# A hybrid decoder layer on one core: projections shared out by the VectorE time of the attention units they stand beside, and three of them moved one phase later

## The chip, the cores and the metric

The kernel is one program on 1 core of one Trainium2 chip. The metric is device time in microseconds (us). The kernel before takes 1305.38 us (median of 3 runs, 1304.23 to 1305.52).

The engines are named as the profile names them: PE is TensorE (matmuls and transposes), PEld its weight load, DVE is VectorE, ACT is ScalarE, POOL is GpSimd, SP is SyncE, which issues the DMAs.

## The reference

One decoder layer, 1024 tokens by 1024 features in float32. One input projection feeds two groups of heads; their outputs go side by side through one output projection, then a layer norm and a gated feed-forward network with a second layer norm.

```python
h = x @ w_in                                    # q, k, v of both groups, and gates
o_diff = diff_attention(dq, dk, dv, ...)        # 4 heads: softmax(q1 k1) - lam * softmax(q2 k2), times v, rms_norm
o_nsa = nsa_attention(nq, ..., gates, ...)      # 8 heads in 2 key groups: compressed + selected + window of 512
mix = concatenate([o_diff, o_nsa]) @ w_out
x = layer_norm(alpha * x + mix)
x = layer_norm(alpha * x + (silu(x @ w_gate) * (x @ w_up)) @ w_down)
```

Every mixer is causal with ALiBi slopes. With 1024 tokens there are 16 selection blocks of 64 and 16 are selected, so the selected branch sees every past key.

## The kernel before, in words

**Arithmetic.** Each float32 operand is split into a high and a low part (a cast on ACT, line L81, and a subtraction on DVE or POOL, L83). A projection is three matmuls per tile, L116, L117 and L118 in `mm3`: high by high, low by high, high by low. They write the PSUM tiles `psM`; `big` and `slot` are buffers for weights and activations, `w` tiles stream through.

**Stages.** First x and the first weights are loaded and the first key group is made (to about 66 us). Then come ten *phases* of attention: four for the sparse heads, which go in pairs (`nsa`, pairs 0 to 3), and six for the differential heads 0 to 3 (`diff`), heads 2 and 3 in two parts each. From about 570 us the rest of the output rows and the feed-forward network run to the end.

**Units.** A sparse phase has 8 blocks of 128 queries with two units each: kind 0 is selected plus compressed, kind 1 is the window. A unit's *front* makes the scores on PE (L323, L326 into `psS`), adds the ALiBi distance and takes the row maximum on DVE (L329, L332, which fill `t` and `m`), exponentiates on ACT (L346) and scales by gate and denominator on POOL (L411). Its *back*, two units later (one later in two of the differential phases), transposes the probabilities on PE (L365 or L355 into `psT`), splits them into `pt` (ACT L81, DVE L83), and multiplies with the values on PE (L418, L426, L428, L481 into `psO`). The differential units combine their two softmaxes on DVE (L466) and POOL (L468), and every four of them are normalised (POOL L496, DVE L497), transposed (L500) and sent through memory (`mix_d`) to the output rows.

**Fillers.** The projections that later phases need are generators, one step per few matmuls: `vg_fill` (values of a sparse block), `qf` (queries of a pair), `kf` (keys of the second sparse group), `kdf`, `qdf`, `dvf` (keys, queries and values of the differential heads), `wo_copy` and `wo_fill` (the output weights, loaded and split), `out_fill` (output rows), `ln_fill`. `held_fill` emits the finish of four differential blocks if it is being held. A key filler ends in DVE work too (L171, two a half), a query filler in DMA moves through `q`.

**What sets the order.** A table `phases` gives for each phase its units, its fillers, how many units a back stands behind its front, a factor `ahead`, a priority and a number `passed`. While the program is written out, `pump` advances the fillers in the middle of each back: before the change in proportion to a unit's *size* (2 x blocks + 1 for sparse units, blocks + 1 in twos for differential ones), so that all the phase's projection matmuls are spread evenly over the sizes. The units still open at the end of a phase have size 0 in the next one, so no filler step stands beside them there. `passed` says past how many later score matmuls a projection may be moved up. A scheduler then puts the instructions of each engine in their final order, with the projections at lower priority (by 2000) than the attention units. Each engine runs its list in that order and waits where an input or a buffer isn't there.

Of the kernel before, what the change touches and what calls it, by code (L numbers as in the profile page):

```python
# [17 lines left out]
P = 128  # L18
# [7 lines left out]
NC = NCMP + 1  # L26
# [11 lines left out]
def layer_kernel(ctx: ExitStack, tc: tile.TileContext, xT, x, w_t, w_vg, w_dv, lam_in, subln,  # L38
# [105 lines left out]
    with ExitStack() as ctx_a:  # L144
# [155 lines left out]


        marks, passed = [], [None]

# [71 lines left out]
        def nsa_units(p, qt, K, V):  # L375
# [7 lines left out]
            def make(i, kind):  # L383
                nb = i + 1 if kind == 0 else min(i + 1, WIN_BLOCKS)
                j0 = i + 1 - nb
                width = nb * P
# [50 lines left out]

                return front, back, 2.0 * nb + 1

# [4 lines left out]
        def diff_units(h, qt, kd, V):  # L444
# [3 lines left out]
            def make(i):  # L448
# [22 lines left out]
                def back(fill):  # L471
# [15 lines left out]
                    done.append(i)  # L487
                    if len(done) == 4:
                        late.append(lambda: finish(orow, ss, state["r0", hf]))

# [16 lines left out]

                return front, back, 2.0 * (i + 1) + 1

# [284 lines left out]
        def held_fill():  # L794

            def steps():
                tc.cur_priority -= FILL_LATER
                finish_held()
                tc.cur_priority += FILL_LATER
                yield 0.0  # L800
            return steps, 0.0

# [4 lines left out]
            ([(nsa, 0, (2, 1, 0, 3, 4, 5, 6, 7))],  # L807
             [vg_fill(3), vg_fill(4), qf(0, 1), vg_fill(5), vg_fill(6), vg_fill(7), qf(1, 0), kf(0), kf(1)],
             2, 1.25, 80, 16),
            ([(nsa, 1, range(8))],  # L810
             [qf(1, 1), wo_copy(0), dvf(0, range(8)), qf(2, 0)], 2, 1, 80, 8),
            ([(nsa, 2, range(7))],
             [qf(2, 1), kdf(0, 0), wo_copy(1), qf(3, 0), kdf(0, 1)], 2, 1, 60, 8),
            ([(nsa, 2, (7,)), (nsa, 3, (1, 0, 2, 3, 5, 4, 6, 7))],
             [qf(3, 1), qdf(0, 0), kdf(1, 0), kdf(1, 1)], 2, 1, 60, 8),
            ([(diff, 0, (2, 1, 0, 3, 5, 4, 6, 7))],
             [qdf(0, 1), qdf(1, 0), dvf(1, range(4))], 1, 1.25, 200, None),
            ([(diff, 1, range(8))],
# [12 lines left out]
        def finish_unit(pump, later):  # L831
            held.extend(late)
            late.clear()
            if pending:
                back, base, size = pending.pop(0)
                tc.cur_priority += later
                back(lambda part: pump and pump(base + part * size))
                tc.cur_priority -= later
            finish_held()

        for parts, fillers, look, ahead, later, passed[0] in phases:
            units = [u for make, head, blocks in parts for u in make(head, blocks)]
            total = sum(u[2] for u in units[:-1])
            rate = sum(f[1] for f in fillers) / total * ahead
            queue = [f[0] for f in fillers]
            run = {"gen": None, "spent": 0.0}

            def step():

                if run["gen"] is None:  # L850
                    if not queue:
                        return False
                    run["gen"] = queue.pop(0)()
                tc.cur_priority += FILL_LATER
# [7 lines left out]

            def pump(at):
                while run["spent"] < at * rate and step():
                    pass

            at = 0.0
            for front, back, cost, needs in units:
                while not needs <= there:
                    assert step()  # L870
                    while run["gen"]:
                        step()
                front()
                pending.append((back, at, cost))
                while len(pending) > look:
                    finish_unit(pump, later)
                at += cost
            while step():
                pass

            pending = [(p[0], 0.0, 0.0) for p in pending]
        while pending or late:
# [388 lines left out]
```

## Time and profile before

| | |
|---|---|
| median of 3 runs | 1305.38 us |
| the profiled execution | 1305.84 us, span 1304.1 us, mean granted TensorE clock 0.999 |
| busy | PE 1286.2 us (99%), PEld 1107.8, DVE 917.8, ACT 652.1, POOL 464.1 |
| pair 0 | 66.4 to 149.3 us |
| pair 1 | 149.3 to 232.8 us |
| pair 2 | 232.8 to 312.0 us |
| pair 3 | 312.0 to 391.2 us |
| differential heads 0, 1 | 391.2 to 482 us |
| differential heads 2, 3 | 482 to 570 us |
| output rows, feed-forward | 570 to 1304 us |

A row of instructions in the trace has start, length, engine, line, operation, output and input names, shapes and count; where the engine was idle ahead of it, the idle time and what ended it stand in brackets. Matmuls overlap in the pipeline, and their shown ends are modelled, so that PE reads as busy almost throughout. A group row ends in busy time, mean ns of one, and the idle time just before its instructions. A row by stretches has the stretch, its length, and for PE, PEld, DVE, ACT and POOL the busy time with the number of instructions, then the granted clock, the DMA share and GB/s.

### The profile page before, as it was taken

How to read it: one execution, taken by the hardware profiler on the slowest of the kernel's cores; microseconds unless marked ns; L12 is line 12 of the kernel's file. 1: busy time of each engine (PE TensorE's matmuls, PEld its weight loads, DVE VectorE, ACT ScalarE, POOL GpSimd, SP SyncE). 2: the span in 40 equal slices, each digit the busy share in tenths (PEclk: the TensorE clock that was granted, in tenths of full speed). 3: DMA queues.
4: the chain of work that ended last, by engine and by line, in shares of the span. 5: the costliest groups of instructions: out<-in, count | busy, mean ns of one | idle time of the engine just before them, and what ended most of it. 6: DMA issues, size and time to landing. Idle time of an engine off the chain costs nothing.

```text
span 1304.1 us, 20490 instructions
## 1 busy us (share of the span) xinstructions
PE 1286.2 (99%) x6955; PEld 1107.8 (85%) x6955; DVE 917.8 (70%) x1963; ACT 652.1 (50%) x1398; POOL 464.1 (36%) x499
## 2 busy tenths in 40 slices
PE   9999999999999999999999999999999999999997
PEld 7998999988988889788887888888888888888886
DVE  5567867778778667774797677776766768555588
ACT  5366866868776566653353333333333335533330
POOL 4434534545435446643613313232231222000071
PEclk9999999999999999999999999999999999999999
DMA  9412012121112135623224566555555559768641
GB/s 354 132 31 62 22 35 62 49 48 48 35 55 70 50 94 149 218 82 113 81 76 149 180 232 228 194 178 173 174 170 185 187 179 346 259 200 291 195 168 65
DMA packets 86841, 183.13 MB, mean 140 GB/s; under 512 B 10576, under 2 KB 19152, under 8 KB 86608
## 3 DMA queue, kind: packets, MB, share of 16 engines
q1 hardware_dynamic: 86736, 181.82, 42.7%
q8 instruction: 55, 0.90, 0.3%
q14 instruction: 50, 0.41, 0.1%
HBM read 116.18 MB, written 57.15 MB: 133 GB/s over the span
## 4 chain that ended last, share of the span: by engine, by line
PE 91%; DVE 4%; DMA 2%; ACT 2%; issue 1%; POOL 0%; SPq 0%; DVEq 0%; ACTq 0%
PE psM L116 11%; PE psM L118 11%; PE psM L117 11%; PE psS L118 6%; PE psS L117 6%; PE psS L116 6%; PE psT L118 5%; PE psT L117 5%; PE psT L116 5%; PE psT L365 4%; PE psS L323 3%; PE psS L326 3%; PE psO L428 2%; PE psO L426 2%; PE psO L481 2%; PE psO L116 2%
## 5 line engine op out<-in xcount | busy, mean ns | idle before, releaser
L346 ACT ACTIVATE t<-t,m 128x384 f32<-128x384 f32 (+7 forms) x192 | 144.2, 752 | 65.4 <-DVE m L332 59.8
L411 POOL TENSOR_SCALAR t<-t,r,gates 128x640 f32<-128x640 f32 (+7 forms) x128 | 99.6, 783 | 180.5 <-DVE r L405 82.4
L116 PE MATMUL psM<-big,w 128*128 128x512 f32 x304 | 120.6, 397 | 0.6 <-DVE slot L171 0.3
L118 PE MATMUL psM<-big,w 128*128 128x512 f32 x304 | 120.1, 396 | 0.0
L117 PE MATMUL psM<-big,w 128*128 128x512 f32 x304 | 119.9, 394 | 0.0
L323 PE MATMUL psS<-slot,q 128*128 128x320 f32 (+10 forms) x304 | 111.8, 369 | 2.2 <-DVE m L332 2.0
L1019 POOL TENSOR_TENSOR half<-half,half 128x512 f32<-128x512 f32 x22 | 33.5, 1524 | 205.0 <-ACT half L1018 205.0
L83 DVE TENSOR_TENSOR pt<-psT,pt 128x512 fp32r<-128x512 f32 (+1 forms) x152 | 91.3, 615 | 13.1 <-ACT pt L81 11.7
L326 PE MATMUL psS<-slot,q 128*128 128x320 f32 (+10 forms) x304 | 99.5, 329 | 0.0
L81 ACT CAST pt<-psT 128x512 fp32r<-128x512 f32 (+1 forms) x152 | 77.3, 525 | 20.6 <-PE psT L365 10.0
L81 ACT CAST big<-slot 128x1024 fp32r<-128x1024 f32 (+1 forms) x54 | 54.4, 1018 | 66.2 <-DVE slot L1011 50.5
L83 DVE TENSOR_TENSOR op<-op 128x1024 fp32r<-128x1024 f32 x44 | 60.9, 1388 | 36.3 <-ACT op L81 35.8
L83 DVE TENSOR_TENSOR big<-slot,big 128x1024 fp32r<-128x1024 f32 (+1 forms) x54 | 63.5, 1182 | 30.5 <-ACT big L81 30.3
L365 PE MATMUL psT<-ident,t 128*128 128x128 f32 x528 | 83.8, 273 | 0.8 <-DVE pt L83 0.7
L81 ACT CAST op<-op 128x1024 fp32r<-128x1024 f32 x44 | 45.9, 1052 | 61.8 <-DMA op<-t_d 55.6
L428 PE MATMUL psO<-pt,slot 128*128 128x256 f32 x264 | 72.1, 294 | 0.1
L426 PE MATMUL psO<-pt,slot 128*128 128x256 f32 x264 | 71.8, 289 | 0.0
L332 DVE CUSTOM_DVE_ANT_0 t<-psS,dsel 128x384 f32<-128x384 f32 (+9 forms) x128 | 62.3, 493 | 13.4 <-PE psS L326 9.6
L1023 POOL TENSOR_TENSOR half<-half,half 128x512 f32<-128x512 f32 x22 | 36.5, 1659 | 99.0 <-DVE half L1022 98.8
L81 ACT CAST big<-big 128x1024 fp32r<-128x1024 f32 (+1 forms) x49 | 44.2, 912 | 45.6 <-DMA big<-t_d 34.0
L118 PEld LDWEIGHTS psM<-big,w 128*128 128x128 f32 x304 | 57.1, 188 | 11.4
L116 PEld LDWEIGHTS psM<-big,w 128*128 128x128 f32 x304 | 57.2, 188 | 11.1 <-ACT w L81 0.8
(371 smaller groups left out, 3971.3 us busy)
## 6 DMA issues: line engine op xcount, KB each, us to landing
a_d<-slot SPq DMA_DIRECT2D x77, 256.0 KB, 3.0
t_d<-slot SPq DMA_DIRECT2D x77, 256.0 KB, 2.2
q<-q SPq DMA_DIRECT2D x48, 256.0 KB, 2.9
slot<-in_w_up_dram SPq DMA_DIRECT2D x22, 512.0 KB, 3.8
slot<-in_w_down_dram SPq DMA_DIRECT2D x22, 512.0 KB, 3.9
op<-a_d SPq DMA_DIRECT2D x44, 256.0 KB, 3.5
op<-t_d SPq DMA_DIRECT2D x44, 256.0 KB, 4.0
big<-a_d SPq DMA_DIRECT2D x33, 256.0 KB, 2.9
```

Source lines behind the costliest of these rows:

```text
L81: nc.scalar.copy(hi, src)
L83: eng.tensor_sub(lo, src, hi.bitcast(F32))
L116: nc.tensor.matmul(acc, lhsT=ah, rhs=bh, start=first, stop=False, skip_group_check=more)
L117: nc.tensor.matmul(acc, lhsT=ah, rhs=bl, start=False, stop=False, skip_group_check=more)
L118: nc.tensor.matmul(acc, lhsT=al, rhs=bh, start=False, stop=last, skip_group_check=more)
L323: mm = nc.tensor.matmul(ps[:, :c + part], lhsT=q[0], rhs=k[:, ks], start=True, stop=False)
L326: nc.tensor.matmul(ps[:, :c + part], lhsT=q[1], rhs=k[:, ks], start=False, stop=True)
L346: nc.scalar.activation(t[:, :width], t[:, :width], AF.Exp, bias=m, scale=-1.0, accum_out=r)
L365: nc.tensor.transpose(tp[:rows, n * P:(n + 1) * P], s, ident)
L411: nc.gpsimd.tensor_scalar(t, t, r[:, c:c + 1], gates[:, i, gc:gc + 1], op0=ALU.mult, op1=ALU.mult)
L426: nc.tensor.matmul(po[:, :256], lhsT=v, rhs=pt[:, 0, n * 256:(n + 1) * 256], start=False, stop=False)
L428: nc.tensor.matmul(po[:, :256], lhsT=v, rhs=pt[:, 1, n * 256:(n + 1) * 256], start=False, stop=last)
```

## The change

Four edits, none of which adds or drops an instruction: each engine has the same work in total.

First, each unit carries an estimate of its own PE and DVE time, from the new helpers `streamed` and `row_ops`, instead of a size. A phase's filler steps are given to a unit by `share`: what PE work would even out the ratio of PE to DVE work over the phase, less the unit's own PE work, and never under 0.2.

Second, units left open at a phase's end keep their estimate, and get filler steps in the next phase; the last units of a phase, whose backs come in the next, don't count in it.

Third, the table. The second group's keys `kf(0)` and `kf(1)` go from pair 0 to pair 1; the first differential values `dvf(0)` with `wo_copy(0)` go from pair 1 to pair 2; the first differential keys `kdf(0, 0)`, `kdf(0, 1)` and `wo_copy(1)` go from pair 2 to pair 3; `kdf(1, 1)` goes from pair 3 to differential head 0. In pair 0 `ahead` goes from 1.25 to 1 and `passed` from 16 to 8.

Fourth, `held_fill` now waits in the queue of fillers until the first halves of all four differential heads are there, and takes the finishes itself.

```diff
+        def streamed(cols, n=1):
+            return n * max(0.105, cols / 2400 + 0.0125)
+        def row_ops(cols, n):
+            return n * 0.24 + 0.00104 * cols
...
-                return front, back, 2.0 * nb + 1
+                cols = width + (0 if kind else NC)
+                n = -(-cols // 512)
+                pe = n * streamed(cols / n, 4) + streamed(P, 2 * nb + 2 * (1 - kind)) + streamed(256, 2 * nb + 1 - kind)
+                dve = 2 * row_ops(width, n) + nb // 2 * 0.69 + nb % 2 * 0.42 + (0.58 if kind else 1.19)
+                return front, back, (pe, dve)
...
                     if len(done) == 4:
+                        there.add(("row", h, hf))
                         late.append(lambda: finish(orow, ss, state["r0", hf]))
...
-                return front, back, 2.0 * (i + 1) + 1
+                n = -(-width // 512)
+                pe = n * streamed(width / n, 4) + streamed(P, i + 1) + streamed(4 * P, i + 1)
+                dve = 2 * row_ops(width, n) + 0.00075 * width + 1.4
+                return front, back, (pe, dve)
...
                 tc.cur_priority -= FILL_LATER
+                held.extend(late)
+                late.clear()
                 finish_held()
                 tc.cur_priority += FILL_LATER
                 yield 0.0
-            return steps, 0.0
+            return steps, 0.0, {("row", h, 0) for h in range(4)}
...
             ([(nsa, 0, (2, 1, 0, 3, 4, 5, 6, 7))],
-             [vg_fill(3), vg_fill(4), qf(0, 1), vg_fill(5), vg_fill(6), vg_fill(7), qf(1, 0), kf(0), kf(1)],
-             2, 1.25, 80, 16),
+             [vg_fill(3), vg_fill(4), qf(0, 1), vg_fill(5), vg_fill(6), vg_fill(7), qf(1, 0)], 2, 1, 80, 8),
             ([(nsa, 1, range(8))],
-             [qf(1, 1), wo_copy(0), dvf(0, range(8)), qf(2, 0)], 2, 1, 80, 8),
+             [qf(1, 1), kf(0), kf(1), qf(2, 0)], 2, 1, 80, 8),
             ([(nsa, 2, range(7))],
-             [qf(2, 1), kdf(0, 0), wo_copy(1), qf(3, 0), kdf(0, 1)], 2, 1, 60, 8),
+             [qf(2, 1), wo_copy(0), dvf(0, range(8)), qf(3, 0)], 2, 1, 60, 8),
             ([(nsa, 2, (7,)), (nsa, 3, (1, 0, 2, 3, 5, 4, 6, 7))],
-             [qf(3, 1), qdf(0, 0), kdf(1, 0), kdf(1, 1)], 2, 1, 60, 8),
+             [qf(3, 1), wo_copy(1), kdf(0, 0), kdf(0, 1), qdf(0, 0), kdf(1, 0)], 2, 1, 60, 8),
             ([(diff, 0, (2, 1, 0, 3, 5, 4, 6, 7))],
-             [qdf(0, 1), qdf(1, 0), dvf(1, range(4))], 1, 1.25, 200, None),
+             [kdf(1, 1), qdf(0, 1), qdf(1, 0), dvf(1, range(4))], 1, 1.25, 200, None),
...
-                back, base, size = pending.pop(0)
+                back, work = pending.pop(0)
                 tc.cur_priority += later
-                back(lambda part: pump and pump(base + part * size))
+                back(lambda part: pump and pump(part, work))
...
-            total = sum(u[2] for u in units[:-1])
-            rate = sum(f[1] for f in fillers) / total * ahead
-            queue = [f[0] for f in fillers]
-            run = {"gen": None, "spent": 0.0}
+            beside = [p[1] for p in pending] + [u[2] for u in units][:-look]
+            given = sum(f[1] for f in fillers)
+            even = (given + sum(pe for pe, _ in beside)) / sum(dve for _, dve in beside)
+            share = lambda w: max(0.2, even * w[1] - w[0])
+            rate = given / sum(map(share, beside)) * ahead
+            queue = [(f[0], f[2] if len(f) > 2 else set()) for f in fillers]
+            run = {"gen": None, "spent": 0.0, "due": 0.0}
...
-                    if not queue:
+                    if not queue or not queue[0][1] <= there:
                         return False
...
-            def pump(at):
-                while run["spent"] < at * rate and step():
+            def pump(part, work):
+                while run["spent"] < run["due"] + part * share(work) * rate and step():
                     pass
+                if part > 0.999:
+                    run["due"] += share(work) * rate
```

The two places below show PE's order; a row has the line, the operation, output and input, the matmul's size and, behind an x, how many stand in a row. Lines from L307 on stand 8 or more lower in the changed kernel: L323 becomes L331, L326 L334, L365 L373, L426 L434, L428 L436, L355 L363, L481 L493 and L500 L513.

The first place is pair 0, block 6, where the selected unit's four score pieces of 480 columns (keys in slot_236) stand among the backs of the units before. Before:

```order
L428 MATMUL psO<-pt,slot_551 128x256
L323 MATMUL psS<-slot_236,q 128x480
L326 MATMUL psS<-slot_236,q 128x480
L365 MATMUL psT<-ident,pc 64x128
L365 MATMUL psT<-ident,t 128x128 x2
L323 MATMUL psS<-slot_236,q 128x480
L326 MATMUL psS<-slot_236,q 128x480
L365 MATMUL psT<-ident,t 128x128 x6
L365 MATMUL psT<-ident,pc 64x128
L323 MATMUL psS<-slot_236,q 128x480
L326 MATMUL psS<-slot_236,q 128x480
```

The same place now:

```order
L436 MATMUL psO<-pt,slot_551 128x256
L373 MATMUL psT<-ident,pc 64x128
L373 MATMUL psT<-ident,t 128x128 x2
L331 MATMUL psS<-slot_236,q 128x480
L334 MATMUL psS<-slot_236,q 128x480
L373 MATMUL psT<-ident,t 128x128 x6
L331 MATMUL psS<-slot_236,q 128x480
L334 MATMUL psS<-slot_236,q 128x480
L116 MATMUL psM<-big,w 128x512
L117 MATMUL psM<-big,w 128x512
L118 MATMUL psM<-big,w 128x512
L116 MATMUL psM<-big,w 128x512
```

Between the third and the fourth score piece there was no projection matmul (psM), and now nine stand there, of which the rows show the first four.

The second place is the end of the differential heads, between the transposes of two finished groups of four blocks (od), those of head 2's and of head 3's first half. Before:

```order
L116 MATMUL psM<-big,w 128x512
L355 MATMUL psT<-ident,t 128x128 x4
L481 MATMUL psO<-slot_5637,pt 128x128 x2
L355 MATMUL psT<-ident,t 128x128 x4
L323 MATMUL psS<-slot_6049,q 128x448
L326 MATMUL psS<-slot_6049,q 128x448
L323 MATMUL psS<-slot_6049,q 128x448
L326 MATMUL psS<-slot_6049,q 128x448
L117 MATMUL psM<-big,w 128x512
L118 MATMUL psM<-big,w 128x512
L116 MATMUL psM<-big,w 128x512
```

The same scores now, from head 2's transposes on:

```order
L513 MATMUL psT<-ident,od 128x128 x4
L363 MATMUL psT<-ident,t 128x128 x9
L331 MATMUL psS<-slot_5973,q 128x448
L334 MATMUL psS<-slot_5973,q 128x448
L493 MATMUL psO<-slot_5519,pt 128x128 x2
L363 MATMUL psT<-ident,t 128x128 x4
L331 MATMUL psS<-slot_5973,q 128x448
L334 MATMUL psS<-slot_5973,q 128x448
L331 MATMUL psS<-slot_5974,q 128x448
L334 MATMUL psS<-slot_5974,q 128x448
```

Before, 18 projection matmuls stand between the two transposes of od, four of them among these rows; now none does, and the next is that of the first output rows, behind head 3's transposes as before.

More of the change, by code (lines that the diff above doesn't have):

```diff
@@ L842, in layer_kernel @@
             units = [u for make, head, blocks in parts for u in make(head, blocks)]
-            total = sum(u[2] for u in units[:-1])
-            rate = sum(f[1] for f in fillers) / total * ahead
-            queue = [f[0] for f in fillers]
-            run = {"gen": None, "spent": 0.0}
+            beside = [p[1] for p in pending] + [u[2] for u in units][:-look]
[5 more added lines that the diff above has]
+            run = {"gen": None, "spent": 0.0, "due": 0.0}
             def step():
                 if run["gen"] is None:
-                    if not queue:
+                    if not queue or not queue[0][1] <= there:
                         return False
-                    run["gen"] = queue.pop(0)()
+                    run["gen"] = queue.pop(0)[0]()
                 tc.cur_priority += FILL_LATER
@@ L861, in step @@
                 return True
-            def pump(at):
-                while run["spent"] < at * rate and step():
-                    pass
-            at = 0.0
-            for front, back, cost, needs in units:
+            def pump(part, work):
+                while run["spent"] < run["due"] + part * share(work) * rate and step():
+                    pass
+                if part > 0.999:
+                    run["due"] += share(work) * rate
+            for front, back, work, needs in units:
                 while not needs <= there:
@@ L873, in layer_kernel @@
                 front()
-                pending.append((back, at, cost))
+                pending.append((back, work))
                 while len(pending) > look:
                     finish_unit(pump, later)
-                at += cost
             while step():
                 pass
-            pending = [(p[0], 0.0, 0.0) for p in pending]
         while pending or late:
```

## The prediction

> **What bounds the kernel now.** The page's first and fourth parts come first.
>
> ```profile
> PE 1286.2 (99%) x6955; PEld 1107.8 (85%) x6955; DVE 917.8 (70%) x1963; ACT 652.1 (50%) x1398; POOL 464.1 (36%) x499
> PE 91%; DVE 4%; DMA 2%; ACT 2%; issue 1%; POOL 0%; SPq 0%; DVEq 0%; ACTq 0%
> ```
>
> PE is on 91% of the chain that ended last, and every engine keeps its work. So the change can only win time in which PE waits inside the attention stage, and the next question is how much of that there is. The busy share hides it: a matmul is shown longer than it keeps PE. The timeline of PE, where no wait is shown, gives the true step from one start to the next.
>
> ```profile
> 301.38 0.60 PE L365 MATMUL psT<-ident,t 128*128 128x128 f32 x4
> 301.81 0.27 PE L365 MATMUL psT<-ident,pc 128*64 128x128 f32 x1
> ...
> 303.46 0.31 PE L326 MATMUL psS<-slot,q 128*128 128x320 f32 x1
> 303.61 0.39 PE L116 MATMUL psM<-big,w 128*128 128x512 f32 x1
> 303.84 0.40 PE L117 MATMUL psM<-big,w 128*128 128x512 f32 x1
> ...
> 305.56 0.28 PE L428 MATMUL psO<-pt,slot 128*128 128x256 f32 x1
> 305.68 0.28 PE L426 MATMUL psO<-pt,slot 128*128 128x256 f32 x1
> ```
>
> 512 columns cost 303.84 - 303.61 = 0.23 us though shown as 0.39; 320 cost 0.15; 256 cost 0.12; 128 cost (301.81 - 301.38) / 4 = 0.108. Sizes between go by columns (480: 0.21, 416: 0.19). Count times step is PE's *work* in a stretch; its length less that is time *lost*. Next the view by stretches, one for each sparse pair (stretch, length, then PE, PEld, DVE, ACT, POOL busy).
>
> ```profile
> 66.20:149.20 83.00, 82.14 (x539) 73.98 (x538) 60.48 (x231) 58.03 (x175) 32.08 (x48) 1.00 0.15 38
> 149.20:232.70 83.50, 83.35 (x631) 79.74 (x630) 58.67 (x209) 60.74 (x166) 38.08 (x55) 1.00 0.17 45
> 232.70:311.90 79.20, 78.33 (x512) 70.55 (x511) 60.92 (x214) 60.09 (x162) 36.45 (x55) 1.00 0.17 41
> 311.90:390.90 79.00, 78.80 (x510) 70.74 (x509) 59.25 (x211) 59.89 (x162) 36.67 (x53) 1.00 0.21 55
> ```
>
> Counting the matmuls of each stretch at their steps (ends taken where the pair's first scores start) gives work of 78.3, 81.7, 74.9 and 75.3 us, so 4.6, 1.8, 4.3 and 3.8 us are lost: 14.5 us. The same count gives 4.1 us for differential head 0, 1.6 for head 1 and some 7.5 for heads 2 and 3; from 570 us on the order hardly changes. All that can be had is thus under 28 us, 2%, and it is spread thin. VectorE is nowhere full over a pair (60.5 of 83.0), so the loss must be local. The worst spot is 119.8 to 138.2 us, blocks 5 and 6 of pair 0; the groups of PE there:
>
> ```profile
> L426 PE MATMUL psO<-pt,slot 128*128 128x256 f32 x19 | 5.3, 294 | 0.0
> L365 PE MATMUL psT<-ident,t 128*128 128x128 f32 x34 | 5.3, 272 | 0.0
> L428 PE MATMUL psO<-pt,slot 128*128 128x256 f32 x18 | 5.2, 312 | 0.0
> L323 PE MATMUL psS<-slot,q 128*128 128x320 f32 x9 | 3.3, 368 | 0.8 <-DVE m L332 0.8
> L326 PE MATMUL psS<-slot,q 128*128 128x320 f32 x8 | 2.5, 309 | 0.0
> ...
> L118 PE MATMUL psM<-big,w 128*128 128x512 f32 x2 | 0.8, 394 | 0.0
> L117 PE MATMUL psM<-big,w 128*128 128x512 f32 x2 | 0.8, 392 | 0.0
> L116 PE MATMUL psM<-big,w 128*128 128x512 f32 x1 | 0.4, 395 | 0.0
> ```
>
> Five projection matmuls in 18.4 us. With the groups left out (2 of 256 columns, 3 of 128, 8 of 480, 8 of 416) the work is 39 x 0.12 + 37 x 0.108 + 17 x 0.15 + 8 x 0.21 + 8 x 0.19 + 5 x 0.23 = 15.6 us, so 2.8 us are lost although PE shows 17.54 busy. What fills the time is the units' own loop, score, VectorE, exponential, transpose:
>
> ```profile
> 119.80:138.20 18.40, 17.54 (x114) 14.79 (x113) 16.80 (x58) 16.21 (x40) 11.30 (x14) 1.00 0.11 35
> 276.10:300.70 24.60, 23.77 (x157) 20.77 (x156) 19.89 (x65) 18.58 (x45) 11.56 (x14) 1.00 0.10 28
> 300.70:315.40 14.70, 14.64 (x106) 13.39 (x105) 13.13 (x51) 13.05 (x36) 6.93 (x8) 1.00 0.06 15
> 379.90:403.60 23.70, 22.77 (x167) 20.48 (x166) 21.89 (x73) 19.19 (x49) 9.45 (x14) 1.00 0.19 40
> ```
>
> There VectorE is busy 16.8 of 18.4 us (91%), against 73% over the pair. The other rows are the further tight spots: the end of pair 2 with the start of pair 3, and the end of pair 3 with the start of differential head 0.
>
> **The change, part by part.** Total work is the same, so each term is lost time taken away or added.
>
> *Blocks 5 and 6 of pair 0.* The changed order has 24 projection matmuls in this stretch instead of 5, 19 x 0.23 = 4.4 us more work; 15.6 + 4.4 = 20.0 us now exceeds VectorE's 16.8, so PE bounds it and the loss goes from 2.8 to near nothing: -2.6 us. If only the loop's length counted, and the projections just lengthened it, the term would be -0.3; I take the end at which PE has 3 us more than any other engine.
>
> *End of pair 2, start of pair 3* (276.1 to 315.4 us). Work before by the same count is 35.2 of 39.3 us, 4.1 lost; the order now has 16 more projection matmuls there, work 38.9. At pair 3's mean rate, 3.8 / 79 = 0.048 us lost per us, 2.0 would be left: -2.1 us (ends 0 and -3.2, the latter at pair 1's rate of 1.8 / 83.5 = 0.022).
>
> *Pair 1 gets tighter.* It gains the key fillers with four VectorE pieces, and loses the value projections, which need none:
>
> ```profile
> L171 DVE TENSOR_TENSOR slot<-psM,slot 64x512 fp32r<-64x512 f32 x12 | 8.3, 689 | 1.1 <-ACT slot L170 0.8
> ```
>
> The row is that of the four sparse pairs, 66 to 391 us. VectorE gets 4 x 0.69 = 2.8 us more, 61.5, while PE's work falls from 81.7 to 74.8: a ratio of 0.82 instead of 0.72, which is what pair 2 has now (60.9 / 74.9 = 0.81, 4.3 lost). So the ends are 0 and +2.5 us. Only blocks 2 and 3, some 14 us, come out with little room; 14 x 0.048 = +0.7 us. Pairs 2 and 3 fall the other way, to 0.71 and 0.73; beside the spots above I give them -0.5 (ends 0 and -2).
>
> *End of pair 3, start of differential head 0* (379.9 to 403.6 us). No filler stands here before or after, and work falls from 20.2 to 19.0 us while VectorE keeps its 21.9. Between 0, if PE's work moved is made up elsewhere, and +1.2: +0.6 us.
>
> *End of the differential heads.* Here the change takes cover away: `dvf(1)`, `qdf(2, 1)` and the output weights stand earlier, and none of the 18 projection matmuls that lay between the two od transposes is left there. What bounds it is read from this stretch and from the chain behind it:
>
> ```profile
> 518.00:550.50 32.50, 29.99 (x181) 25.38 (x180) 23.32 (x70) 20.89 (x52) 21.58 (x20) 1.00 0.66 211
> ...
> 544.47 1.05 POOL ss L496
> 545.54 1.39 DVE od L497
> 547.07 0.64 PE psT L500 x4
> ...
> 548.24 1.91 DMA mix_d<-tmp
> 550.17 3.56 DMA w<-mix_d
> 553.75 0.63 ACT w L81
> 554.42 0.50 PE psM L116
> ```
>
> From head 3's transposes to the first output row's matmul, 554.42 - 547.07 = 7.35 us pass whatever PE does. Now 6.4 us of units' work stand in their place, before 4.9: 1.5 us less lost, the lower end. The upper end has VectorE set the pace: its 23.3 us for the same units and then the 7.35, 30.65, against 20.9 us of PE work left, so 9.8 lost, where 518.0 to 554.42 loses 36.4 - 30.5 = 5.9 now: +3.9 us. The order shows also that the second `wo_fill`'s POOL work moves:
>
> ```profile
> 530.79 8.88 POOL L83 TENSOR_TENSOR big<-big 128x512 fp32r<-128x512 f32 x7 [0.32 <-ACT big L81]
> ```
>
> One of these takes 8.88 / 7 = 1.27 us; they now stand ahead of head 2's last first-half scaling, L468, and of head 3's L496, both of which must wait out up to 7 of them. No row excludes either end; the middle is +1.2 us.
>
> Two rows of VectorE show what such POOL work does to a neighbour:
>
> ```profile
> 412.10 1.70 DVE L466 SCALAR_TENSOR_TENSOR t<-t,r 128x480 f32<-128x480 f32 x1
> 467.07 0.72 DVE L466 SCALAR_TENSOR_TENSOR t<-t,r 128x480 f32<-128x480 f32 x1
> 410.76 2.53 POOL L83 TENSOR_TENSOR w<-w 128x512 fp32r<-128x512 f32 x2
> ```
>
> The first runs into POOL's pieces and takes 0.98 us longer. [...] I leave it out, since VectorE there has room if PE sets the pace.
>
> *Sum:* -2.6 - 2.1 + 0.7 - 0.5 + 0.6 + 1.2 = -2.7 us. The profiled execution took 1305.84 us, of which the span is 1304.1; it would take 1303.1. It lies 0.46 above the median of 1305.38, from which the forecast is **1302.7 us**.
>
> **The rivals.** *The loss only changes places.* If a pair's loss follows its mean ratio of VectorE to PE work, the pairs swap: 0.77, 0.72, 0.81, 0.79 with 4.6, 1.8, 4.3, 3.8 lost become 0.81, 0.82, 0.71, 0.73 with 4.3, 4.3, 1.8, 1.8 and the 0.7 of pair 1: 12.9 instead of 14.5, -1.6; with the differential end's 1.2 that is -0.4, **1305.0**. For it speaks that pair 1, the one with most PE work, loses least; against it that the loss in pair 0 sits in one spot that is now filled.
>
> *The differential end becomes VectorE's.* The place is head 2's and 3's second parts, the price +3.9 us from above, and it decides once it exceeds what the sparse pairs win; with nothing won there, **1309.3**, slower. For it speaks that VectorE (23.3), ACT (20.9) and POOL (21.6) all exceed the 15.5 us of PE work that stay beside these units in 518.0 to 550.5; against it that the projections now come ahead of them, so that VectorE can run on while PE does those.
>
> *Every sparse pair falls to pair 1's rate.* The row for it is the first stretch of pair 1, where PE waits for nothing that shows:
>
> ```profile
> 149.20:222.70 73.50, 73.50 (x564) 70.89 (x563) 49.43 (x175) 52.14 (x145) 35.41 (x52) 1.00 0.15 40
> ```
>
> The four pairs' work is 71.5 + 74.8 + 81.3 + 83.0 = 310.6 us; at 0.022 that loses 6.8, with 2.5 for the seam to head 0 9.3 instead of 14.5: -5.2, and -1.5 from the differential end's lower bound: **1298.7**. Against it: VectorE's share is only 67% in this row, and 71 to 82% in the changed pairs.
>
> That the change doesn't level the fill at all is ruled out by the order of pair 0.
>
> **How the numbers follow.** Forecast 0.40, loss changes places 0.29, differential end slower 0.15, pair 1's rate everywhere 0.16. A difference under 0.2%, 2.6 us, can't be told from none: faster is under 1302.8, slower over 1308.0. The forecast lies at that bound, so of its 0.40 I count 0.22 as faster, 0.17 same, 0.01 slower; the first rival gives 0.04, 0.22, 0.03; the second 0, 0.02, 0.13; the third 0.15, 0.01, 0. Faster 0.41, same 0.42, slower 0.17. The forecast's own range is 1300.9 to 1304.5; the whole range goes from 1298.0, below the third rival, to 1307.8, which leaves out most of the second.
>
> **What would show it.** In the changed profile pair 0 should end about 9 us earlier than now (6.8 us of its work is moved, 2.6 regained), with some 24 projection matmuls in the stretch of the 480- and 416-column scores, and VectorE under 85% busy there. Pair 1's length less its work should be between 1.8 and 4.3 us. From head 2's od transposes,
>
> ```profile
> 529.85 0.60 PE L500 MATMUL psT<-ident,od 128*128 128x128 f32 x4
> ```
>
> to head 3's at 547.07 it is 17.2 us now; the same time of the changed kernel shows whether VectorE sets the pace: at about 17.2 - 18 x 0.23 = 13 us PE sets it and the lower end holds; at 17 us or more, the upper one. The prediction is wrong if pair 0 still loses over 3 us, or if the differential heads from 482 us on take 3 us more than their work explains.

## The result, and the profile after

The changed kernel takes 1313.12 us (median of 4 runs, 1311.15 to 1316.19) against 1305.44: a ratio of 1.0065, interval 1.0052 to 1.0077. It is slower, and outside the forecast's range. The profiled execution took 1311.15 us, the shortest of the four, with a span of 1309.4 us: 5.3 more than before. The page's first and fourth parts:

```profile
PE 1285.4 (98%) x6955; PEld 1109.7 (85%) x6955; DVE 917.3 (70%) x1963; ACT 651.4 (50%) x1398; POOL 464.5 (35%) x499
PE 88%; DVE 6%; DMA 2%; issue 1%; ACT 1%; POOL 1%; SPq 0%; DVEq 0%; ACTq 0%
```

The counts are the same, PE's share of the chain is 3 points lower and VectorE's 2 higher. The sparse pairs by themselves (same columns as before) went as hoped:

```profile
66.10:140.70 74.60, 73.80 (x509) 68.10 (x508) 57.55 (x227) 54.88 (x171) 29.83 (x46) 1.00 0.15 36
140.70:216.90 76.20, 76.20 (x531) 71.09 (x529) 61.10 (x214) 60.46 (x163) 39.27 (x56) 1.00 0.19 50
216.90:300.00 83.10, 82.74 (x609) 78.83 (x608) 57.59 (x207) 60.07 (x164) 36.97 (x53) 1.00 0.18 46
300.00:386.60 86.60, 85.99 (x549) 77.31 (x547) 63.14 (x218) 62.81 (x169) 37.39 (x55) 1.00 0.19 50
```

With PE's work of 71.5, 74.8, 81.3 and 83.0 us they lose 3.0, 1.4, 1.8 and 3.5 us, 9.7 in all instead of 14.5. Differential head 0 starts at 386.6 instead of 390.9 us. Then the lead is lost, and more, in three places. The table gives PE's lost time (length less count times step, as in the prediction; the steps are those of `streamed`, 0.226 us for 512 columns and 0.105 for 128) between equal amounts of PE work from the span's start, so that kernels with different orders can be set side by side; work 440 lies in differential head 1, 440 to 500 covers the first parts of heads 2 and 3 with the start of the second, 500 to 560 the rest of them, 560 to 660 in the output rows and the start of the feed-forward network. The other columns are experiments told below: "phase 6 old" is the changed kernel with the old rule in phase 6, "phase 6 new" the sparse-only kernel with the new rule there.

| PE work | before | changed | sparse only | diff. only | ahead 1.8 | values first | weights on VectorE | phase 6 old | phase 6 new | phases 6, 7 old |
|---|---|---|---|---|---|---|---|---|---|---|
| 0 to 440 | 27.0 | 22.3 | 22.5 | 26.7 | 22.1 | 22.6 | 22.2 | 22.5 | 22.6 | 22.2 |
| 440 to 500 | 2.0 | 6.4 | 2.1 | 9.6 | 6.1 | 4.7 | 6.0 | 6.3 | 2.7 | 6.5 |
| 500 to 560 | 6.6 | 10.5 | 5.8 | 10.7 | 7.2 | 11.0 | 7.8 | 6.6 | 7.3 | 5.6 |
| 560 to 660 | 3.9 | 5.7 | 3.9 | 5.6 | 4.1 | 5.7 | 4.0 | 4.0 | 4.0 | 4.0 |
| sum | 39.6 | 44.9 | 34.3 | 52.7 | 39.6 | 44.0 | 40.0 | 39.4 | 36.5 | 38.3 |

So the changed kernel has -4.7, +4.4, +3.9 and +1.8 us, which with rounding is the 5.3 of the span.

**First place, head 3's queries.** The chain of waits through 500 us (start, length, what), and the PE row at its end:

```profile
496.98 0.67 DVE q L177
497.67 0.47 SPq L161
...
498.19 7.79 DMA q<-q
506.00 4.58 DMA q<-q
...
510.62 0.33 PE L331 MATMUL psS<-slot,q 128*128 128x128 f32 x1 [2.53 <-DMA q<-q]
```

A query filler ends on VectorE (L177) and in three DMA moves, the third of which waits for the first two. Here they take 12.9 us from the first one's issue to the third one's landing, where before they took 7.1, and PE waits 2.53 us for them though 72 value matmuls stand in between. SyncE's own rows show what else is under way. Before:

```profile
495.92 4.67 SPq L161 DMA_DIRECT2D q<-q  x3
500.80 0.50 SPq L99 DMA_DIRECT2D w<-mix_d  x1
502.99 0.34 SPq L592 DMA_DIRECT2D slot<-in_x_dram  x1
503.42 1.11 SPq L161 DMA_DIRECT2D q<-q  x2
```

After:

```profile
495.93 0.90 SPq L99 DMA_DIRECT2D big<-wo_d  x2
496.93 0.37 SPq L608 DMA_DIRECT2D slot<-in_x_dram  x1
497.67 1.11 SPq L161 DMA_DIRECT2D q<-q  x2
498.87 0.88 SPq L608 DMA_DIRECT2D slot<-in_x_dram  x1
499.85 10.62 SPq L161 DMA_DIRECT2D q<-q  x4
```

Before, the three moves go out together, and head 2's next queries follow 7.5 us later. Now both query fillers end at nearly the same time, and their six moves are mixed with each other, two loads of x and two of the output weights. (Of the x4 row, the first two moves and the last are head 2's, the third is head 3's.)

**And the clock behind it.** The stretches around that wait (the last three numbers are the granted clock, the DMA share and GB/s):

```profile
508.00:510.60 2.60, 0.09 (x1) 0.00 (x0) 0.00 (x0) 1.09 (x4) 0.00 (x0) 1.00 0.23 54
510.60:512.00 1.40, 1.38 (x11) 1.38 (x12) 0.53 (x4) 0.57 (x3) 0.00 (x0) 1.00 0.71 143
512.00:515.40 3.40, 3.40 (x19) 3.40 (x18) 0.69 (x3) 0.31 (x2) 0.73 (x2) 0.52 0.84 178
515.40:518.00 2.60, 2.60 (x19) 2.43 (x19) 1.14 (x6) 1.80 (x8) 0.00 (x0) 0.98 0.76 306
```

From 1.5 us after the wait PE ran for 3.4 us at half clock, which costs another 3.4 x 0.48 = 1.6 us and shows in no wait. The two together, 4.1, are all but 0.3 of this place.

**Second place, POOL and VectorE at the end.** Three rows of VectorE before the change:

```profile
518.48 0.63 DVE L466 SCALAR_TENSOR_TENSOR t<-t,r 128x320 f32<-128x320 f32 x1
519.03 0.15 DVE L493 TENSOR_TENSOR r<-r 128x4 f32<-128x4 f32 x1
523.82 0.16 DVE L495 SCALAR_TENSOR_TENSOR ss<-ss,r 128x4 f32<-128x4 f32 x1
```

After, the second output weights' pieces on POOL, the same three operations beside them, and what follows:

```profile
525.92 7.78 POOL L83 TENSOR_TENSOR big<-big 128x512 fp32r<-128x512 f32 x6
530.16 1.17 DVE L478 SCALAR_TENSOR_TENSOR t<-t,r 128x320 f32<-128x320 f32 x1
531.25 1.23 DVE L506 TENSOR_TENSOR r<-r 128x4 f32<-128x4 f32 x1
532.81 0.91 DVE L508 SCALAR_TENSOR_TENSOR ss<-ss,r 128x4 f32<-128x4 f32 x1
535.65 1.03 POOL L509 TENSOR_TENSOR ss<-ss,mhalf 128x4 f32<-128x4 f32 x1
...
538.35 0.66 PE L513 MATMUL psT<-ident,od 128*128 128x128 f32 x4 [0.44 <-DVE od L510]
551.95 0.63 PE L513 MATMUL psT<-ident,od 128*128 128x128 f32 x4
559.07 0.39 PE L116 MATMUL psM<-big,w 128*128 128x512 f32 x1
```

Two operations on 4 columns take 1.23 and 0.91 us. L508 belongs to head 2's normalisation; L506 is the first step of head 3's and stands ahead of it in VectorE's order. The chain of waits to head 2's od transposes at 538.35 runs through both. POOL's own step of that normalisation (L509) also stands behind the pieces, in POOL's order, and starts 1.9 us after L508 has ended. From 538.35 on it is 13.6 us to head 3's transposes and 7.1 more to the first output row. **Third place:** the output rows and norms between about 670 and 695 us lose 1.8 us more; the chain of waits runs mostly through VectorE there from 664.7 to 677.2 us.

### The profile page after: what moved, and what is told of

Read it like the earlier page. It is cut to its first block, busy times and chain, and to the rows that moved or that the text cites. A ratio compares the mean times of both kernels' runs of the same rounds, so it can differ in the third digit from the quotient of the medians.

```text
span 1309.4 us, 20509 instructions
## 1 busy us (share of the span) xinstructions
PE 1285.4 (98%) x6955; PEld 1109.7 (85%) x6955; DVE 917.3 (70%) x1963; ACT 651.4 (50%) x1398; POOL 464.5 (35%) x499
## 4 chain that ended last, share of the span: by engine, by line
PE 88%; DVE 6%; DMA 2%; issue 1%; ACT 1%; POOL 1%; SPq 0%; DVEq 0%; ACTq 0%
PE psM L116 10%; PE psM L118 10%; PE psM L117 10%; PE psT L118 5%; PE psT L117 5%; PE psT L116 5%; PE psS L117 5%; PE psS L118 5%; PE psS L116 5%; PE psT L373 5%; PE psS L331 3%; PE psS L334 3%; PE psO L436 2%; PE psO L434 2%; PE psO L493 2%; PE psO L118 2%
## 5 line engine op out<-in xcount | busy, mean ns | idle before, releaser
L331 PE MATMUL psS<-slot,q 128*128 128x320 f32 (+10 forms) x304 | 111.5, 369 | 6.4 <-DVE m L340 3.4
L334 PE MATMUL psS<-slot,q 128*128 128x320 f32 (+10 forms) x304 | 99.2, 329 | 0.0
L373 PE MATMUL psT<-ident,t 128*128 128x128 f32 x528 | 83.6, 272 | 0.1
L1041 POOL TENSOR_TENSOR half<-half,half 128x512 f32<-128x512 f32 x22 | 36.5, 1660 | 101.2 <-DVE half L1040 101.0
L434 PE MATMUL psO<-pt,slot 128*128 128x256 f32 x264 | 72.3, 289 | 0.0
L436 PE MATMUL psO<-pt,slot 128*128 128x256 f32 x264 | 71.6, 292 | 0.0
L331 PEld LDWEIGHTS psS<-slot,q 128*128 128x128 f32 x304 | 57.7, 190 | 14.3 <-DVE m L340 8.4
L118 PEld LDWEIGHTS psM<-big,w 128*128 128x128 f32 x304 | 57.1, 188 | 11.7 <-POOL w L83 0.2
```

Of the source, the lines that this page charges most:

```text
L118: nc.tensor.matmul(acc, lhsT=al, rhs=bh, start=False, stop=last, skip_group_check=more)
L331: mm = nc.tensor.matmul(ps[:, :c + part], lhsT=q[0], rhs=k[:, ks], start=True, stop=False)
L334: nc.tensor.matmul(ps[:, :c + part], lhsT=q[1], rhs=k[:, ks], start=False, stop=True)
L373: nc.tensor.transpose(tp[:rows, n * P:(n + 1) * P], s, ident)
L434: nc.tensor.matmul(po[:, :256], lhsT=v, rhs=pt[:, 0, n * 256:(n + 1) * 256], start=False, stop=False)
L436: nc.tensor.matmul(po[:, :256], lhsT=v, rhs=pt[:, 1, n * 256:(n + 1) * 256], start=False, stop=last)
```

## The experiments

Most kernels choose between the two rules phase by phase. Phases count from 0; 0 to 3 are the sparse pairs, 4 and 5 differential heads 0 and 1, 6 and 7 the first parts of heads 2 and 3, 8 and 9 their second parts. A unit's work then holds its old size as a third number, `w[2]`. The edit to the changed kernel (left out is the rule of the change; the old `held_fill` goes with old shares in phase 8):

```diff
-        for parts, fillers, look, ahead, later, passed[0] in phases:
+        for ph, (parts, fillers, look, ahead, later, passed[0]) in enumerate(phases):
...
+            if ph in BY_TIME:
...
+            else:
+                beside = [u[2] for u in units[:-1]]
+                pending = [(p[0], (0.0, 0.0, 0.0)) for p in pending]
+                share = lambda w: w[2]
```

**The two halves.** First the change in the sparse phases alone, `BY_TIME = [0, 1, 2, 3]` with the new table and the old `held_fill`.

> The change in the four sparse phases only (new table, new shares there); from differential head 0 on the shares go by the old sizes, and the held finish is emitted as before, so that from the od transposes of head 0 on PE's projections stand as in the kernel before (18 between head 2's and head 3's od). Theory A, two independent halves: the profile of the changed kernel has lost 4.5 us less than before by 440 us (22.2 against 26.7) and all of its extra loss after 500 us, so this one should take 1305.4 - 4.5 = 1301 us (1300 to 1302.5), with about 35 us lost by 560 us less 4.5, that is 30. Rival B, the end is set by something that does not start earlier when PE arrives earlier (transfers, POOL): the 4.5 us are given back in the differential heads and the time is 1304 to 1306.

Measured: 1300.22 us (5 runs, 1299.51 to 1300.52), ratio 0.9966 (0.9953 to 0.9979). Theory A holds: the 4.7 us are kept to the end. This version is faster than both kernels.

The other half, `BY_TIME = [4, 5, 6, 7, 8, 9]`, old table, new `held_fill`:

> The other half alone: the old table and the old shares in the sparse phases, the new shares from differential head 0 on, with the held finish waiting for the first halves of all four heads; no projection stands between the od transposes of heads 2 and 3. Theory A: 1305.4 plus the extra loss between 500 and 560 us (38.3 - 23.9 = 14.4 against 34.6 - 28.5 = 6.1, so 8.3) plus 1.7 at the start of the feed-forward network: 1315 us (1312 to 1318). Rival B: the changed kernel meets these waits only because it arrives 4.5 us earlier; then this one loses about 4 to 5 and takes 1309 to 1310.

Measured: 1319.39 us (4 runs, 1316.15 to 1320.27), ratio 1.011 (1.0095 to 1.0124). The loss is in this half, above the range expected, and larger without the sparse half than with it. PE waits 4.6 us for head 3's queries here. The wait itself has a mean clock of 0.90 (by an estimate from it, half clock in the last 4.6 x 0.10 / 0.50 = 0.9 us), and the clock stays at 0.50 for 5.9 us behind it:

```profile
512.50:517.10 4.60, 0.00 (x0) 0.00 (x0) 0.00 (x0) 0.98 (x4) 0.00 (x0) 0.90 0.49 108
517.10:523.00 5.90, 5.90 (x27) 5.90 (x28) 1.29 (x7) 0.98 (x4) 0.73 (x2) 0.50 0.57 131
523.00:525.00 2.00, 2.00 (x17) 1.92 (x16) 0.98 (x5) 1.18 (x4) 0.00 (x0) 1.00 0.96 389
```

**What wins in the sparse phases.** The new table with the old shares (`BY_TIME = []`), the new shares with the old table (`BY_TIME = [0, 1, 2, 3]`), and the sparse-only kernel with `passed` back at 16:

```diff
-             [..., vg_fill(7), qf(1, 0)], 2, 1, 80, 8),
+             [..., vg_fill(7), qf(1, 0)], 2, 1, 80, 16),
```

> The new table of phases alone, with the old shares by size everywhere (and the old finish). Blocks 5 and 6 of pair 0 get 27 projection matmuls by their order, where before had 4 and the change has 18. If the gain of the sparse phases comes from the table (the second group's keys out of pair 0 and no early spending there), 1301 to 1302.5. If it comes from the shares by VectorE time, little is left here: 1304 to 1305.5.

> The new shares in the four sparse phases alone, with the old table (and the old shares from differential head 0 on). Blocks 5 and 6 of pair 0 get 19 projection matmuls. If the gain comes from the shares, 1301 to 1302.5; if it comes from the table, 1304 to 1305.5. If a pair's loss goes by its mean ratio of VectorE to PE work, nothing changes here: 1305.

> The sparse-only kernel (1300.2) with passed in pair 0 back at 16, as before the change. By the order, blocks 5 and 6 of pair 0 then have 9 projection matmuls instead of 18 (4 before the change). If the projections beside these blocks are what regains the 2 us of pair 0, about half of that is lost again: 1301 to 1301.5. If the order within pair 0 doesn't matter so long as its total work falls, 1300 to 1300.5.

Measured: table alone 1304.64 us (0.9999, 0.999 to 1.0009), shares alone 1302.52 (0.9982, 0.9973 to 0.9992), sparse-only with `passed` at 16 1302.82 (0.9984, 0.9975 to 0.9994). The shares alone give about half of the gain, the table alone nothing, both together 4.7. The number `passed` was underrated: 2.1 us are lost again by PE work 140, more than pair 0 had regained, not half of it. The table alone puts 27 projection matmuls beside blocks 5 and 6, more than the change does, and yet 11.8 us are lost by PE work 140, as before (11.9; 10.4 in the changed kernel). So filling the tightest spot is not enough.

**The queries and the cover.** In the changed kernel, one number for phase 6:

```diff
-             [kdf(3, 0), kdf(3, 1), qdf(3, 0)], 2, 1.25, 130, None),
+             [kdf(3, 0), kdf(3, 1), qdf(3, 0)], 2, 1.8, 130, None),
```

> The changed kernel with one number altered: the factor ahead of the first four blocks of differential head 2 from 1.25 to 1.8, so that head 3's first queries are complete before head 2's next ones start. Their three DMA moves then stand together ahead of the x loads again (in the changed kernel two moves, an x load, four moves of both), and 12 projection matmuls stand between the od transposes of heads 2 and 3 instead of none. Theory A, the slow end comes from two things, head 3's queries arriving late (2.5 us of wait and 1.7 us of slow TensorE clock in the profile) and the missing cover (9.4 us lost from 528 to 554 us against 5.8): the first is gone and most of the second, so 1301 to 1303. Rival B, the new shares make the end slow in other ways (more VectorE and POOL work in the same stretch): still 1308 or more.

Measured: 1305.78 us (1.0005, 0.9995 to 1.0014). Against the expectation, the second place and the output rows recover (7.2 and 4.1) but the queries are still late by 2.45 us. Their last step on VectorE (L177) starts at 492.79 us, and PE is ready for head 3's first score 5.9 us later, where the sparse-only kernel leaves 8.2 us; the three moves, in order this time, need 8.3 us from L177 to their landing. Again PE ran at a clock of 0.50, for 3.4 us behind the wait.

Next the two fillers of phase 7 exchanged:

```diff
-             [qdf(2, 1), dvf(1, range(4, 8))], 2, 1.25, 60, None),
+             [dvf(1, range(4, 8)), qdf(2, 1)], 2, 1.25, 60, None),
```

> The changed kernel with the two fillers of head 3's first four blocks exchanged: the values of the second pair before head 2's second queries. Head 3's first queries are then moved alone (three moves in a row, though behind two x loads), with 67 value matmuls (8 us) between their last projection and the first score; no projection stands between the two od transposes, as in the changed kernel. Theory A: the wait for the queries gets shorter or goes, the missing cover stays; 1306 to 1310, by so much slower than the sparse-only kernel (1300.2) as the cover is worth, 4 to 8. If the wait for the queries is the whole matter, 1301 to 1302; if DMA load and not the order of the moves makes it, 1312 or more.

Measured: 1310.39 us (1.0039, 1.0024 to 1.0054), as theory A had it. The wait for the queries shrinks to 1.64 us, with no slow clock behind it:

```profile
505.00:508.00 3.00, 1.36 (x13) 1.15 (x10) 0.07 (x1) 1.42 (x4) 0.00 (x0) 1.00 0.80 183
508.00:512.00 4.00, 4.00 (x24) 3.39 (x23) 1.13 (x7) 1.15 (x5) 0.73 (x2) 1.00 1.04 363
```

The second and third place stay as bad as in the changed kernel (11.0 and 5.7), so they don't come from the queries.

**POOL's pieces.** The changed kernel with the second output weights split on VectorE:

```diff
-                    wo[nh, kp] = load_split_here(wo_d[nh, kp], *big_tiles(), l_eng="pool", order=(0, 1))
+                    wo[nh, kp] = load_split_here(wo_d[nh, kp], *big_tiles(), l_eng="pool" if nh == 0 else "dve", order=(0, 1))
```

> The changed kernel with the second output weights' eight subtractions on VectorE instead of POOL, so that POOL's 7.8 us block ahead of the normalisations of the differential end is gone, and VectorE has 8 x 0.8 = 6.6 us more there. The queries still arrive late, and nothing stands between the two od transposes. If VectorE sets the pace of the end (theory A), this is slower than the changed kernel by 3 to 6: 1316 to 1319. If POOL's block is what holds the end, it is faster by 2 to 4: 1309 to 1311.

Measured: 1308.46 us (1.0028, 1.0017 to 1.004): 4.7 faster than the changed kernel, though VectorE has eight operations of about 0.7 us more to do. That VectorE's amount of work sets the pace is refuted; what held the end was POOL's block. The same VectorE operations in this kernel:

```profile
532.52 0.74 DVE L478 SCALAR_TENSOR_TENSOR t<-t,r 128x320 f32<-128x320 f32 x1
533.18 0.15 DVE L506 TENSOR_TENSOR r<-r 128x4 f32<-128x4 f32 x1
531.24 0.15 DVE L508 SCALAR_TENSOR_TENSOR ss<-ss,r 128x4 f32<-128x4 f32 x1
```

The three take 1.04 us instead of 3.31, 2.3 less, where the second place gains 2.7 (10.5 to 7.8). The edit also frees POOL's own queue for L509, so it doesn't separate the two effects; that the collisions are the larger part is argued from the chain. The third place recovers too (4.0), which the trace shows but this experiment doesn't explain. The same edit to the sparse-only kernel:

> The sparse-only kernel (1300.2) with the second output weights' eight subtractions on VectorE instead of POOL. In that kernel POOL's 8.9 us block stands in a stretch where head 2's and 3's scalings with two SBUF inputs don't run beside it. If the pieces on POOL only hurt the changed kernel by where they stand, this gains nothing and pays some of the 5.4 us of VectorE time: 1300 to 1302.5. If POOL's block is a cost in itself wherever it stands, 1297 to 1299.

Measured: 1301.56 us (0.9973, 0.9963 to 0.9984), 1.3 slower than without. So POOL's block is no cost in itself. Before the change too a VectorE operation collides with it (L464 on one column takes 1.05 us at 538.63 us, 0.22 at 503.49), and in the sparse-only kernel POOL's next step waits 0.19 us behind the block for the same operation (L476 there); but what it costs there is less than moving the pieces.

**Which phase.** One phase back to the old shares, `BY_TIME` all but 6, and that one phase alone added to the sparse ones, `[0, 1, 2, 3, 6]`:

> The changed kernel with the old shares by size in one phase only, the first four blocks of differential head 2 (which make head 3's first queries). Their moves then lead head 3's first scores as before, 12 projection matmuls stand between the two od transposes, and POOL's eight weight pieces stand behind head 3's normalisation instead of ahead of it. Theory: the changed kernel's end pays three things, the queries (2.5 us of wait and the slow clock behind it, 4.5), POOL's pieces colliding with VectorE and what follows at the output rows (4.5, from the kernel with those pieces on VectorE), and the cover (some 1.5 to 2). Then only the last is left: 1301 to 1302.5. If the shares of the other differential phases cost by themselves, 1304 or more.

> The sparse-only kernel (1300.2) with the new shares in that one phase too, the first four blocks of differential head 2. Head 3's first scores then stand some 2 us of PE work behind the last projection of its queries, as in the kernel with ahead at 1.8, where PE waited 2.45 us for them and ran at half clock behind it (3.65 lost). Theory: this one phase is what makes the queries late, so 1300.2 + 3.6 + 1 to 2 for the five projections less between the od transposes: 1304 to 1306. If the queries' lateness needs the following phases' shares too, 1300 to 1302.

Measured: 1305.53 us (1.0007, 0.9997 to 1.0017) and 1302.94 (0.9984, 0.9974 to 0.9993), both against the expectation. With phase 6 back the second and third place are as before the change (6.6 and 4.0), but the queries are late by 2.65 us although PE has done their projections by the same time as in the sparse-only kernel (490.9 us at the latest). With phase 6 alone they are late by only 0.45, and 1.5 us are lost in the second place, where the cover is thinner (13 projections between the od transposes instead of 18; 7.3 against 5.8). The reason for the lateness is in VectorE's order. The sparse-only kernel:

```profile
490.93 0.75 DVE L177 SCALAR_TENSOR_TENSOR q<-psM,qscale,q 128x512 fp32r<-128x512 f32 x1 [1.34 <-ACT q L176]
492.52 0.38 DVE L478 SCALAR_TENSOR_TENSOR t<-t,r 128x160 f32<-128x160 f32 x1
```

The kernel with phase 6 back:

```profile
488.82 3.77 POOL L83 TENSOR_TENSOR big<-big 128x512 fp32r<-128x512 f32 x3
491.49 1.11 DVE L476 SCALAR_TENSOR_TENSOR r<-r,lam,r 128x1 f32<-128x1 f32 x1
492.64 0.38 DVE L478 SCALAR_TENSOR_TENSOR t<-t,r 128x160 f32<-128x160 f32 x1
492.94 0.74 DVE L177 SCALAR_TENSOR_TENSOR q<-psM,qscale,q 128x512 fp32r<-128x512 f32 x1
```

The queries' last step on VectorE stands behind a unit's combination instead of ahead of it, 2.0 us later. Some 0.9 of the 2.0 is again a collision: L476 on one column ends with POOL's third piece after 1.11 us. (The kernel with `ahead` at 1.8 has the same order there.) The moves themselves then take 0.9 us longer, and there is no slack to take either up. Set side by side, from the start of L177, in us:

| | before | sparse only | changed | values first | ahead 1.8 | phase 6 old | phase 6 new |
|---|---|---|---|---|---|---|---|
| PE ready for head 3's first score after | 8.5 | 8.2 | 11.2 | 9.4 | 5.9 | 6.3 | 7.6 |
| third move landed after | 7.9 | 7.9 | 13.7 | 11.0 | 8.3 | 8.8 | 7.9 |
| PE waits | 0 | 0 | 2.53 | 1.64 | 2.45 | 2.65 | 0.45 |

So the queries are late for two reasons. In the changed kernel PE leaves them more time than before, but the moves land 5.8 us later; about half of that goes when head 2's moves are out of the way (values first). With `ahead` at 1.8 or phase 6 back the moves are nearly as quick as before, but VectorE starts them too late. Even before the change they had only 0.6 us to spare, and 0.3 in the sparse-only kernel. (The expectation for phase 6 alone puts 2 us of PE work between the queries' projections and the score; by the trace it is some 8.)

A last kernel asks whether anything else in the new shares costs, `BY_TIME` all but 6 and 7:

> The changed kernel with the old shares by size in two phases, the first four blocks of differential heads 2 and 3; the new shares stay in the sparse phases, heads 0 and 1 and the second parts of heads 2 and 3, and the held finish still waits for all four heads' first halves. By the order 18 projections stand between the two od transposes again, and POOL's eight weight pieces stand behind head 3's normalisation. If the loss lies in these two phases' shares alone, with the queries' lead of about 7.5 us restored, this equals the sparse-only kernel: 1300 to 1301. If the new shares of heads 0 and 1 or of the last two phases, or the gate on the held finish, cost anything, 1302 to 1305. In a kernel with only the first of the two phases put back, the queries were still late by 2.65 us, because VectorE's part of them stood behind the first head-3 unit's combination; where that happens here too, 1304 to 1305.

Measured: 1304.66 us (0.9997, 0.9988 to 1.0007). The cover, POOL's pieces and the output rows are as in the sparse-only kernel (5.6 and 4.0; the pieces stand behind head 2's L509 again, and ahead of head 3's), so the second and third place do come from phases 6 and 7. What is left is the one case the expectation set apart:

```profile
492.81 0.74 DVE L177 SCALAR_TENSOR_TENSOR q<-psM,qscale,q 128x512 fp32r<-128x512 f32 x1
501.75 0.45 PE L331 MATMUL psS<-slot,q 128*128 128x128 f32 x1 [2.80 <-DMA q<-q]
```

2.8 us of wait and a clock of 0.50 for 3.4 us behind it make 4.5 us, about all of the 4.4 us by which this kernel's first place (6.5) is worse than the sparse-only one's (2.1). Left open: a kernel of the changed order with the queries alone on time wasn't tried.

## Why the prediction was wrong

**The sparse phases were right in sum.** Forecast -3.9 us, measured -4.7, kept to the end by the sparse-only kernel at 1300.22. Pair by pair the loss after is 3.0, 1.4, 1.8 and 3.5, sum 9.7, where the terms gave 10.6. Blocks 5 and 6 of pair 0 are now filled (18 projection matmuls between the first 416- and the last 480-column score, where 4 stood, with VectorE at 11.66 of 14.70 us, 79%):

```profile
107.20:121.90 14.70, 14.44 (x92) 12.59 (x89) 11.66 (x44) 11.39 (x31) 6.17 (x8) 1.00 0.29 64
```

Pair 0 as a whole regained 1.7 us, not 2.6. The term of +0.7 for pair 1 did not come: it lost 1.4 with VectorE at 61.10 of 74.8 us of PE work, the very ratio of 0.82 at which pair 2 lost 4.3 before. So the first rival's rule, loss by a pair's mean ratio, is wrong; how the fill is spread within a pair counts, and the table alone shows that one filled spot doesn't do it. One thing in the working doesn't come out as printed: the work of 78.3, 81.7, 74.9 and 75.3 us, and with it the 14.5 lost, goes by steps of 0.226 and 0.105 us; by the printed 0.23 and 0.108 only 8.9 us would be lost. The level hangs on the step, the differences between kernels don't.

**The differential end was mis-sized, and for the wrong reason.** The term was +1.2 between -1.5 and +3.9; measured +3.9 in the second place. The upper end was worked out from VectorE's 23.3 us as the pace, and 528.5 to 559.1 did take 30.6 us where that end had 30.65:

```profile
528.50:559.10 30.60, 25.73 (x154) 19.87 (x154) 25.50 (x81) 19.92 (x51) 20.81 (x19) 1.00 0.37 104
```

Yet more VectorE work with less on POOL made it faster, so the agreement is an accident. Some 2.3 to 2.7 us go with POOL's pieces; the remaining 1.2 to 1.6 goes with the missing cover, which no run isolates. The prediction had such a collision before it, the row of 1.70 us against 0.72, and left it out because VectorE had room. That was the wrong test: among the operations held was a step of the normalisation on which the od transposes wait. It also has the pieces ahead of head 3's L496; they stood ahead of that before the change too, and what they moved ahead of is head 2's (L509 now). The prediction's own sign for the end, 13 us between the two od transposes, came (13.6) and said nothing, since most of the loss lay ahead of the first of them. Its other sign, over 3 us more than their work explains in the differential heads from 482 us on, came true.

**The step that failed** is the sentence that `dvf(1)`, `qdf(2, 1)` and the output weights "stand earlier". It was priced as cover taken away, and nothing was set down for what they are moved past: head 3's queries, whose last projections, VectorE step and three DMA moves now end together with head 2's and behind the loads, so that they land 5.8 us later. That is +4.4 us, 1.6 of it the slow clock, for which there was no term. The output rows' +1.8 had no term either; it goes with POOL's block (5.6 or 5.7 in each profiled kernel with the block ahead of head 2's L509, 3.9 to 4.1 in the others), and how is open.

The second rival had the right place and 3.9 us, but its condition, nothing won in the sparse phases, did not hold. The medians differ by 7.7 us and the profiled runs by 5.3; the changed kernel's runs spread over 5 us and the sparse-only kernel's over 1. The run of 1316.19 us had a mean granted clock of 0.994 and the other three 0.998, so more time at a low clock is, by an estimate from these means, part of that run's excess; what made the one of 1314.70 longer is not shown, as only one run was profiled.

## What to carry to other kernels

When work is moved earlier in an order, follow its outputs through every queue to the first reader, and compare the lead with the measured landing time: here three chained moves of 256 KB landed 7.1 to 8.1 us after the first one's issue when they went out in a row, 10.2 behind loads and 12.9 or more mixed with three others. With 0.3 to 0.6 us to spare, 2 us of VectorE order and 0.9 of slower moves cost 4.4 us. Levelling one ratio won time in the sparse phases, where PE waits mostly for the units' own loop; in the differential ones, where its longest single wait is for a transfer (2.53 us), it lost. There the due times of the transfers have to be in the rule as well. Try such a rule stage by stage: one half of this change is worth -4.7 us, the other cost 12 to 13 on top of it.

## What the runs showed of the hardware

In the profiled runs PE's clock dropped to half after the waits of 2.45, 2.53, 2.65 and 2.80 us for head 3's queries (`ahead` at 1.8, the changed kernel, phase 6 old, phases 6 and 7 old), at once or up to 1.5 us after PE had resumed, and stayed there for about 3.4 us. After the wait of 4.62 us, in the kernel with the other half alone, it stayed at 0.50 for 5.9 us. A wait of 1.64 us (in the kernel with the values first) left it at 1.00, and so did one of 2.36 us at the start of the changed kernel's span. So a wait of 2.53 us came to 4.1 us in the changed kernel. What sets the drop and its length is not shown.

A VectorE operation on 4 columns took 0.15 us with none of POOL's subtractions beside it (L493 at 519.03 us before the change) and 1.23 us beside them (the same operation, L506, at 531.25 us after it). There it ends at 532.48 us, within 0.1 us of the end of POOL's fifth piece (525.92 + 5 x 7.78 / 6 = 532.40, an estimate from the row of six), so that its length is not its own.
